# Hybrid attention and convolution trunk: values and compression with 64 stationary columns and two heads in turn, transposes in two banks, the conformer's statistics and the output banks placed anew

## The chip, the cores and the metric

The kernel runs on one core of one Trainium2 chip, as one launch over the whole trunk. The metric is the device time of a run in microseconds (us); the number quoted for a kernel is the median of three runs. Beside the runs stands one profiled execution, in which the hardware profiler recorded the instructions of every engine. The engines are PE (TensorE, matmuls; PEld is its weight loads), DVE (VectorE), ACT (ScalarE), POOL (GpSimd) and SP (SyncE, which here only queues the DMAs of the weights). Matmul results land in eight banks of PSUM, here bank 0 to bank 7; in the lists of instructions further down they are named bank_64 to bank_71.

## What is computed

One layer on 256 tokens of 2048 channels, in float32:

```
h    = rms_norm(x, mix_norm_g)
proj = h @ w_in                      # q 1024, k/v of 3 branches x 4 kv heads x 64, gates 48, conv 2048 columns
attn = nsa_attention(q, kv, sigmoid(gates), rel_bias, cmp_pos, cmp_w1, cmp_w2)   # 16 q heads, 4 kv heads
conv = conformer_conv(conv_in, conv_w, conv_b, conv_ln_g, conv_ln_b)
x    = x + concat([attn, conv]) @ w_out
x    = x + conv_glu_ffn(rms_norm(x, ffn_norm_g), w_up, ffn_conv_w, ffn_conv_b, w_down)
out  = rms_norm(x, final_norm_g)

def compress_tokens(tok, pos, w1, w2):     # blocks of 32 tokens, a step of 16 apart: 15 blocks a head
    blocks = <overlapping blocks of tok> + pos
    return silu(flat(blocks) @ w1) @ w2

def conformer_conv(h2, conv_w, conv_b, ln_g, ln_b):
    a, gate = split(h2, 2)
    u = causal_depthwise_conv(a * sigmoid(gate), conv_w, conv_b)    # 31 taps, 1024 channels
    return silu(layer_norm(u, ln_g, ln_b))                          # mean and variance over the channels
```

The attention of each head is the gated sum of three softmax attentions, all with a bias by relative position: over the 15 compressed blocks, over selected blocks of 64 tokens, and over a window. At 256 tokens all blocks are selected and the window covers everything, so the last two differ only in their keys and values.

## The kernel before

**Arithmetic.** Every large projection is done in high and low parts: a value is split into a part `h` rounded to the matmul's format and the rest `l`, and a product is three matmuls, h·h, h·l and l·h (`mm3`, lines L142 to L144; rows form in L149 to L151, and L615 to L617 for the values and gates). Such a matmul is one record in the trace. Plain float32 matmuls (value products, transposes by an identity, statistics) may show as two records, "passes". The weights come in chunks of 1 MB through SP's queue; ACT rounds them (`wh`, L110) and DVE or, for chunks 5 to 30, POOL makes the rest (`wl`, L115), some of it between the matmuls of the chunk ahead.

**Order.** PE's order is written out by hand. It takes the chunks in turn: 16 for the conformer's gates and values (GLU), 4 for the keys and values that get compressed, 4 for the other keys (k), 2 for the values of one branch (v), 4 for the values of the other with the gates (vg), 8 for the queries (q), 16 for the output projection (each a quarter of the output columns `qr` by a group `g` of 4 k-tiles, in an order `OUT_ORDER`), then 88 and 44 for the feed-forward part. `w_next` brings in the next chunk and runs what was left for "late", the copies out of the banks of the chunk before.

Each chunk calls `hook` four times. A hook runs: the attention ticks that `TICKS` gives it; what stands in `behind`; one piece of a weight split; one `step`, which takes one entry each from the lists `conf` (the conformer's statistics) and `steps` (compression, the compressed branch, residuals); and `fill`, which issues convolution taps while a running estimate of DVE's clock is not far ahead of PE's. An empty entry (`lambda: None`) in a list delays what is behind it by one hook.

**Convolution.** For each of 8 blocks of 128 channels, 30 taps are DVE instructions (L368) on an accumulator in bank 6 or 7; the last one writes `y[:, j]`. As soon as no tap is left, `conf_steps` starts the layer norm: `conf_sum` reduces `y` over the 8 blocks on DVE (L426), the mean is two matmuls against `inv_c` (L430), then subtract (L457), square on ACT, reduce again, the variance by four small matmuls (L437), a power on POOL (L467), a diagonal (L443), spread over the rows by two matmuls (L446), a multiply. Later come the SiLU and the split into `cf["o"]`. All of these use one corner of bank 6.

**Compression.** `cmp_in` (L517) multiplies the 16 position pairs of all four heads against the k weights and the v weights side by side: 128 stationary columns and 150 moving ones (75 for k, 75 for v), of which two diagonal quarters are used. The moving columns are picked out of `tok` with a step of 8. `cmp_sig` and `cmp_silu` form the hidden layer `hd`, `cmp_out` the second step (L540 for k, L544 for v).

**Attention** is a pipeline over 32 units: 8 pairs of heads `i`, the head `r` of the pair, the branch `br`. Tick n issues, in this order: `st_out` of unit n-6, `st_transpose` of n-5 (three transposes into bank 6), `st_scores` of n (banks 2, 4, 5), `st_rec` of n-3, `st_min` of n-1 (bias and row minimum, DVE), `st_evac` of n-5 (ACT's copy `es` of the transposed weights, 2 buffers), `st_scale` of n-3 (POOL), `st_exp` of n-1 (ACT). `st_out` is two value matmuls into bank 7: the stationary is `v[:, 0]`, 128 columns wide, in which `vt` holds the 64 values of head r and 64 zeros, so that the two heads of a pair add up in the upper and the lower rows of bank 7. The pair's last unit adds the compressed branch and splits bank 7 into `ma_h` and `ma_l`.

The compressed branch has its scores (`cmp_scores`) and the transposes of its weights `pcb` (`cmp_tr`, L685) in bank 3. The output projection's rows are in banks 0 and 1, 2 and 3, 4 and 5, 6 and 7 (`ob`); attention runs on into its first chunks, and loops ahead of output chunks 1, 3 and 6 force what is still left.

## Time and profile before

| | |
|---|---|
| runs | 1134.94 us median of 3 (1134.56 to 1135.63) |
| profiled execution | span 1135.5 us |
| PE | 1113.0 us busy, 98% of the span, 6482 matmul records |
| PEld | 976.3 us busy, 86% |
| DVE | 768.0 us busy, 68%, 1252 instructions |
| ACT | 579.2 us busy, 51%, 836 instructions |
| POOL | 187.1 us busy, 16%, 144 instructions |
| HBM | 204.27 MB read, 182 GB/s over the span |

The record of the profiled execution names no time for it beyond its span, so this is its own time; it lies 0.6 us above the median of the runs. How to read the rows: matmuls are pipelined, so the duration of one (some 0.28 us for 256 columns) is longer than the distance between the starts of two (0.12 us), and it is the distance that PE's path is made of. In a list in order of time the columns are the start and the duration in us, the engine, the line, the operation, what it writes and reads, its shape (stationary rows by columns, then rows by moving columns) and, in brackets, how long the engine had been idle and what it waited for. `xN` at a row's end counts the records taken together.

### The profile page before, as it was taken

To read this page: it belongs to the slowest core of one execution; us is meant where nothing else is said; L and a number is where in the kernel's file an instruction comes from. 1 tells how busy PE (TensorE), PEld (TensorE's weight loads), DVE (VectorE), ACT (ScalarE), POOL (GpSimd) and SP (SyncE) were. 2 spreads that over 40 slices of the span, in tenths; PEclk is the share of its full clock that TensorE was granted. 3 is DMA by queue.
4 is the path that set the end of the run, shared out by engine and by line. 5 is a ranking of instruction groups with operands and counts; after the bars stand their busy time and mean duration, and the time that the engine had idled before them with its cause. 6 is when DMAs were issued, how large, how long until landed. Compare 5 with 4: busy or idle time off the path is not lost.

```text
span 1135.5 us, 16238 instructions
## 1 busy us (share of the span) xinstructions
PE 1113.0 (98%) x6482; PEld 976.3 (86%) x6482; DVE 768.0 (68%) x1252; ACT 579.2 (51%) x836; POOL 187.1 (16%) x144
## 2 busy tenths in 40 slices
PE   8999997999999999999999999999999999999997
PEld 8999997999788888888888888888888888888886
DVE  7699676766455677777777777777777645556554
ACT  7444255677564555555545555554555444444442
POOL 0888666356500000000000000000000000000000
PEclk9999998999999999999999999999999999999999
DMA  9585424422354555555555555555555454555541
GB/s 374 212 289 207 159 89 153 146 75 111 120 215 156 210 199 195 197 194 186 185 186 190 188 193 198 191 190 185 186 185 191 182 191 182 195 185 188 188 165 75
DMA packets 32425, 207.46 MB, mean 183 GB/s; under 512 B 3883, under 2 KB 6203, under 8 KB 8284
## 3 DMA queue, kind: packets, MB, share of 16 engines
q1 hardware_dynamic: 28972, 199.85, 48.7%
q10 hardware_dynamic: 3376, 6.55, 1.6%
q8 instruction: 51, 0.84, 0.3%
q14 instruction: 26, 0.21, 0.1%
HBM read 204.27 MB, written 2.12 MB: 182 GB/s over the span
## 4 chain that ended last, share of the span: by engine, by line
PE 91%; DVE 4%; ACT 2%; POOL 1%; issue 1%; DMA 1%; SPq 0%; DVEq 0%; POOLq 0%; ACTq 0%
PE bank L976 29%; PE bank L994 21%; PE bank L978 14%; PE bank L142 5%; PE bank L144 5%; PE bank L143 5%; PE bank L151 3%; PE bank L149 3%; PE bank L150 3%; DVE bank L368 2%; PE bank L766 1%; PE bank L753 1%; DMA hb<-in_head 1%; PE bank L517 1%; POOL wl L115 1%
## 5 line engine op out<-in xcount | busy, mean ns | idle before, releaser
L110 ACT ACTIVATE wh<-wraw 128x2048 fp32r<-128x2048 f32 (+2 forms) x239 | 355.6, 1505 | 375.7 <-issue 143.8
L115 DVE TENSOR_TENSOR wl<-wraw,wh 128x2048 fp32r<-128x2048 f32 (+1 forms) x185 | 363.3, 1970 | 201.8 <-ACT wh L110 201.6
L976 PE MATMUL bank<-xt,wh 128*128 128x512 f32 x1408 | 488.6, 394 | 0.0
L978 PE MATMUL bank<-xt,wl 128*128 128x256 f32 x1408 | 390.1, 277 | 0.0
L976 PEld LDWEIGHTS bank<-xt,wh 128*128 128x128 f32 x1408 | 264.0, 188 | 61.1
L978 PEld LDWEIGHTS bank<-xt,wl 128*128 128x128 f32 x1408 | 264.4, 188 | 0.0
L142 PE MATMUL bank<-xt,wh 128*128 128x256 f32 x512 | 147.6, 288 | 2.5 <-ACT wh L243 2.5
L144 PE MATMUL bank<-xt,wl 128*128 128x256 f32 x512 | 145.8, 285 | 0.3 <-DVE wl L244 0.2
L143 PE MATMUL bank<-xt,wh 128*128 128x256 f32 x512 | 145.5, 284 | 0.0
L178 POOL TENSOR_TENSOR rstd<-ms,half 128x1 f32<-128x1 f32 x4 | 2.2, 553 | 821.0 <-DVE ms L171 821.0
L115 POOL TENSOR_TENSOR wl<-wraw,wh 128x1024 fp32r<-128x1024 f32 (+1 forms) x54 | 121.1, 2272 | 43.0 <-ACT wh L110 42.0
L994 PE MATMUL bank<-wh,gl 128*128 128x512 f32 x336 | 106.0, 396 | 0.0
L994 PE MATMUL bank<-wh,gh 128*128 128x512 f32 x336 | 106.0, 396 | 0.0
L994 PE MATMUL bank<-wl,gh 128*128 128x512 f32 x336 | 106.0, 396 | 0.0
L142 PEld LDWEIGHTS bank<-xt,wh 128*128 128x128 f32 x512 | 98.5, 192 | 4.2 <-ACT wh L243 2.9
L144 PEld LDWEIGHTS bank<-xt,wl 128*128 128x128 f32 x512 | 98.3, 192 | 0.7 <-DVE wl L244 0.7
L143 PEld LDWEIGHTS bank<-xt,wh 128*128 128x128 f32 x512 | 98.5, 192 | 0.5
L368 DVE SCALAR_TENSOR_TENSOR bank<-us,cw,bank 128x256 f32<-128x256 f32 x232 | 95.4, 482 | 3.5 <-ACT bank L363 2.9
L939 DVE SCALAR_TENSOR_TENSOR yt<-u,vecs,yt 128x255 f32<-128x255 f32 (+1 forms) x176 | 80.9, 480 | 3.1
L994 PEld LDWEIGHTS bank<-wh,gl 128*128 128x128 f32 x336 | 63.3, 188 | 15.4
L994 PEld LDWEIGHTS bank<-wl,gh 128*128 128x128 f32 x336 | 63.3, 188 | 15.4
L994 PEld LDWEIGHTS bank<-wh,gh 128*128 128x128 f32 x336 | 63.2, 188 | 15.4
(191 smaller groups left out, 1117.1 us busy)
## 6 DMA issues: line engine op xcount, KB each, us to landing
wraw<-in_w_u SPq DMA_DIRECT2D x88, 1024.0 KB, 4.8
wraw<-in_w_d SPq DMA_DIRECT2D x44, 1024.0 KB, 4.7
wraw<-in_w_t SPq DMA_DIRECT2D x30, 1024.0 KB, 4.9
wraw<-in_w_o SPq DMA_DIRECT2D x16, 1024.0 KB, 4.8
wraw<-in_w_vg SPq DMA_DIRECT2D x4, 608.0 KB, 3.8
hb<-in_head SPq DMA_DIRECT2D x2, 1024.0 KB, 10.3
xr<-in_x SPq DMA_DIRECT2D x2, 1024.0 KB, 18.9
wb<-rel_scratch ACTq DMA_DIRECT2D x1, 2048.0 KB, 10.8
```

The source lines that it names most:

```text
L110: nc.scalar.activation(h[:, sl], raw[:, sl], AF.Copy)
L115: (nc.gpsimd if pooled else nc.vector).tensor_sub(l[:, sl], raw[:, sl], h[:, sl].bitcast(F32))
L142: nc.tensor.matmul(ps, wh, xh, start=first, stop=False)
L143: nc.tensor.matmul(ps, wh, xl, start=False, stop=False)
L144: nc.tensor.matmul(ps, wl, xh, start=False, stop=last)
L149: nc.tensor.matmul(ps, xh, wh, start=first, stop=False)
L150: nc.tensor.matmul(ps, xh, wl, start=False, stop=False)
L368: nc.vector.scalar_tensor_tensor(y[:, j] if last else acc[0], us[:, j, k:k + T], cw[:, j, k:k + 1], acc[0], op0=OP.mult, op1=OP.add)
L939: nc.vector.scalar_tensor_tensor(ys[i][:, d:], us_[i][:, :T - d], fcw[:, c, k:k + 1], ys[i][:, d:], op0=OP.mult, op1=OP.add)
L976: nc.tensor.matmul(bk[i], wh[:, k, sl], xt[:, kt].rearrange("p a t -> p (a t)"), start=kt == 0, stop=False)
L978: nc.tensor.matmul(bk[i][:, :T], wl[:, k, sl], xt_h[:, kt], start=False, stop=kt == KD - 1)
L994: nc.tensor.matmul(banks[n], g[p][:, kt % 4, sl], ws[w][:, k * 1024 + n * 512:k * 1024 + (n + 1) * 512], start=kt + i == 0, stop=i == 2 an ...
```

## The change

- **Values.** `vt` loses its zeros; a stationary is 64 columns wide. `st_out` does nothing for r = 0, and for r = 1 it issues the products of both heads, in turn, into rows 0 to 63 and 64 to 127 of bank 7: four matmuls a branch, eight passes. Since it needs both heads' `es`, it comes a tick later (DEEP = 7), and `es` has 5 buffers instead of 2.
- **Compression.** `cmp_in` does the same with k and v: 32 matmuls of 64 stationary and 75 moving columns in place of 16 of 128 and 150. It stands behind 6 empty steps instead of 2, and `cmp_out` behind 5 instead of 1.
- **Transposes** go to banks 3 and 6 in turn. The compressed branch moves its scores to bank 1 and its transposes to bank 0 (bank 5 for the last group, m = 3, which also gets two empty steps instead of none ahead of its transposes).
- **Conformer's statistics.** `ysum` is added up on DVE as each block's taps end (`conf_add`). `conf_center` is put in ahead of q chunk 1: one matmul for the mean (both halves of the tokens at once, bank 0, `ones` with the factor in ACT's copy), subtraction in four pieces, squares by ACT in four pieces, added up by DVE. `conf_norm` is put in ahead of output chunk 2: variance (two matmuls against a column of `ones`), power, diagonal, one spread matmul, all in bank 6, with empty steps between; then multiply, SiLU and split.
- **Output banks.** `ob` becomes (0,1), (4,2), (5,3), (6,7); output chunks have their own ticks in `TICKS`, and the forcing loops become assertions.
- **Small tiles.** The table of the feed-forward taps, `fcw`, gets a tile of its own and is loaded at the start of the feed-forward part, on ACT's queue ahead of `gfin`; `inv_c` and the clearing of the zeros in `vt` (POOL) are gone.

```
-        vt = ap.tile([P, 2, 2, 2, 3, HD], F32, name="vt")
-        nc.gpsimd.memset(vt[:, :, :, :, 1], 0.0)
+        vt = ap.tile([P, 2, 2, 2, 2, HD], F32, name="vt")
...
         def st_out(n):
             i, r, br = units[n]
-            es = US.pop(n)
-            o, v = bank[7], vt[:, :, br, i // 4, r:r + 2]
+            if r == 0:
+                return
+            es, o, q = [US.pop(n - 2), US.pop(n)], bank[7], i // 4
             kw = dict(skip_group_check=True)
-            nc.tensor.matmul(o[:, :T], v[:, 0], es[:, :T], start=r + br == 0, stop=False, **kw)
-            nc.tensor.matmul(o[:, P:T], v[:, 1], es[:, T:], start=False, stop=False, **kw)
-            if r == 1 and br == 1:
+            for b, cols in enumerate((slice(0, T), slice(P, T))):
+                for rr in range(2):
+                    nc.tensor.matmul(o[64 * rr:64 * rr + 64, cols], vt[:, b, br, q, rr],
+                                     es[rr][:, :T] if b == 0 else es[rr][:, T:], start=br + b == 0, stop=False, **kw)
+            if br == 1:
...
-        DEEP = D_T + 1
+        DEEP = D_T + 2
...
             for i in range(16):
-                nc.tensor.matmul(bank[4][:, :150], w1[:, i].rearrange("p v d -> p (v d)"), tok[:, :, :, i:i + 113:8],
-                                 start=i == 0, stop=i == 15)
+                for kv in range(2):
+                    nc.tensor.matmul(bank[4][64 * kv:64 * kv + 64, :75], w1[:, i, kv], tok[:, kv, :, i:i + 113:8],
+                                     start=i == 0, stop=i == 15)
...
-        steps.extend((lambda: None, lambda: None, cmp_in, lambda: None, lambda: cmp_sig(0), lambda: cmp_sig(1),
-                      lambda: cmp_silu(0), lambda: cmp_silu(1), lambda: None, cmp_out, lambda: None, cmp_keep))
+        steps.extend((*[lambda: None] * 6, cmp_in, lambda: None, lambda: cmp_sig(0), lambda: cmp_sig(1),
+                      lambda: cmp_silu(0), lambda: cmp_silu(1), *[lambda: None] * 5, cmp_out, lambda: None, cmp_keep))
...
+        def conf_add(j):
+            summed.append(j)
+            if len(summed) > 1:
+                nc.vector.tensor_add(ysum, y[:, summed[0]] if len(summed) == 2 else ysum, y[:, j])
...
+        def conf_mean():
+            cf["b"] = bank[0][:, :T]
+            nc.tensor.matmul(cf["b"], ones, ysum, start=True, stop=True)
+            conf_keep(1.0 / NCONV)
...
+        def conf_center():
             conf.extend((
-                lambda: None, lambda: conf_sum("y", y, 0, P), lambda: conf_sum("y", y, P, T), lambda: None,
-                lambda: None, lambda: conf_mean(0), lambda: conf_mean(1),
-                lambda: (conf_apply(OP.subtract, 0), conf_sq(0)), lambda: conf_apply(OP.subtract, 4),
...
+                no, no, conf_mean, no, lambda: conf_apply(OP.subtract, 0), lambda: conf_apply(OP.subtract, 2),
+                lambda: conf_sq(0, 0), lambda: (conf_sq(2, 2), conf_apply(OP.subtract, 4)),
+                lambda: conf_apply(OP.subtract, 6), lambda: conf_fold(2, 2),
+                lambda: conf_sq(4, 2), no, lambda: conf_fold(2, 2), lambda: conf_sq(6, 2), no,
+                lambda: conf_fold(2, 2), no, lambda: conf_fold(1, 1)))
+        def conf_norm():
+            conf.extend((
+                no, no, conf_var, no, conf_rstd, no, conf_diag, no, conf_spread, no,
...
-            es = wk.tile([P, 384], F32, name="es", bufs=2)
-            nc.scalar.activation(es, bank[6][:, :384], AF.Copy)
+            es = wk.tile([P, 384], F32, name="es", bufs=5)
+            nc.scalar.activation(es, bank[TR_BANKS[n % 2]][:, :384], AF.Copy)
...
-        TICKS = {0: {}, 1: {2: 1, 3: 1}, 2: {0: 1, 1: 1, 2: 1, 3: 1}, 3: {0: 1, 1: 2, 2: 1, 3: 2}}
+        TICKS = {0: {}, 1: {2: 1, 3: 1}, 2: {0: 1, 1: 1, 2: 1, 3: 1}, 3: {0: 1, 1: 1, 2: 1, 3: 2}, 4: {0: 1, 1: 1, 2: 1, 3: 2}, 5: {0: 1, 1: 1, 2: 1}}
...
-            if i == 2:
+            if i == 1:
                 fill(1e9)
+                conf_center()
...
-        ob = [bank[0:2], bank[2:4], bank[4:6], bank[6:8]]
+        ob = [[bank[b] for b in p_] for p_ in ((0, 1), (4, 2), (5, 3), (6, 7))]
...
+        fcw = fp.tile([P, 2 * NFT, 4], F32, name="fcw")
+        nc.scalar.dma_start(fcw.rearrange("p t k -> p (t k)"), a["vecs"][:, KD:])
```

In the lists below a row is an instruction: its line, operation, what it writes and reads, and its shape (for a matmul, stationary columns by moving columns; otherwise partitions by elements); x6 stands for six alike in a row.

**Place 1, the mean of the layer norm.** PE before: the mean (L430) stands among the value-and-gate matmuls of the vg chunks (L615 to L617).

```order
L617 MATMUL bank_67<-wh,xt 128x304
L430 MATMUL bank_70<-y,inv_c 128x128
L615 MATMUL bank_66<-wh,xt 128x304
L616 MATMUL bank_66<-wl,xt 128x304
L617 MATMUL bank_66<-wh,xt 128x304
```

PE now: it stands in q chunk 1 (L142 to L144), behind the first scores of attention (L712, L713).

```order
L144 MATMUL bank_65<-xt,wl 128x256
L712 MATMUL bank_66<-k_h,qs 128x256
L713 MATMUL bank_66<-k_l,qs 128x256
L712 MATMUL bank_68<-k_h,qs 128x512
L713 MATMUL bank_68<-k_l,qs 128x512
L430 MATMUL bank_64<-ysum,ones 128x256
L142 MATMUL bank_65<-xt,wh 128x256
```

So it moved past the rest of vg and q chunk 0, and covers both halves of the tokens at once.

DVE before, at the end of the convolution: the last taps of the last two blocks (L368, writing `y`), then the reductions over the blocks (L426) and the subtraction (L457).

```order
L368 SCALAR_TENSOR_TENSOR bank_71<-us,cw,bank_71 128x256
L368 SCALAR_TENSOR_TENSOR y<-us,cw,bank_70 128x256
L368 SCALAR_TENSOR_TENSOR bank_71<-us,cw,bank_71 128x256 x6
L368 SCALAR_TENSOR_TENSOR y<-us,cw,bank_71 128x256
L426 TENSOR_REDUCE y<-y 128x128 x2
L457 TENSOR_TENSOR y<-y,ck 128x1024 x2
```

DVE now, at the same end of the convolution (the taps are L369 here, the addition L354); behind it come the small operations of the gates.

```order
L369 SCALAR_TENSOR_TENSOR y<-us,cw,bank_70 128x256
L354 TENSOR_TENSOR ysum<-ysum,y 128x256
L369 SCALAR_TENSOR_TENSOR bank_71<-us,cw,bank_71 128x256 x6
L369 SCALAR_TENSOR_TENSOR y<-us,cw,bank_71 128x256
L354 TENSOR_TENSOR ysum<-ysum,y 128x256
L626 TENSOR_SCALAR alive<-wb 128x1
L627 TENSOR_SCALAR gates<-gates,alive 128x16
```

The two reductions are replaced by an addition behind the last tap of each block but the first, and the subtraction is no longer next in line.

**Place 2, the values.** PE before, a tick of attention inside a q chunk: the value matmuls (L766, L767), the transposes (L753), the scores (L711, L712).

```order
L144 MATMUL bank_65<-xt,wl 128x256
L766 MATMUL bank_71<-es,vt 128x256
L767 MATMUL bank_71<-es,vt 128x128
L753 MATMUL bank_70<-ident,e 128x128 x3
L711 MATMUL bank_66<-k_h,qs 128x256
L712 MATMUL bank_66<-k_l,qs 128x256
L711 MATMUL bank_69<-k_h,qs 128x512
L712 MATMUL bank_69<-k_l,qs 128x512
L142 MATMUL bank_65<-xt,wh 128x256
```

PE now, a tick with values (L770; the transposes are L754).

```order
L144 MATMUL bank_65<-xt,wl 128x256
L770 MATMUL bank_71<-es,vt 64x256 x2
L770 MATMUL bank_71<-es,vt 64x128 x2
L754 MATMUL bank_67<-ident,e 128x128 x3
L142 MATMUL bank_65<-xt,wh 128x256
```

Two units' value matmuls now stand together, 64 columns wide, and the transposes go to bank 3 or bank 6; scores follow in every second tick with values (not in this one), and ticks without values remain between them.

**Place 3, the second step of compression.** PE before: `cmp_out` (L540, L544) stands in a k chunk.

```order
L143 MATMUL bank_66<-xt,wh 128x256
L144 MATMUL bank_66<-xt,wl 128x256
L540 MATMUL bank_69<-hd,w_101 64x30 x2
L544 MATMUL bank_68<-w_101,hd 32x64 x8
L142 MATMUL bank_66<-xt,wh 128x256
```

PE now: it stands among the value matmuls of v (L601 to L603).

```order
L602 MATMUL bank_65<-wl,xt 128x256
L603 MATMUL bank_65<-wh,xt 128x256
L541 MATMUL bank_69<-hd,w_99 64x30 x2
L545 MATMUL bank_68<-w_99,hd 32x64 x8
L601 MATMUL bank_64<-wh,xt 128x256
```

It moved back by the eight empty steps that were added ahead of it, four of them ahead of the first step: two chunks.

More of the change, by code (lines that the diff above doesn't have):

```diff
@@ L338, in hook @@
             fill(1.0 if i in ticks else 0.8 if cbst["q"] else 2.0)
-            if not side and cbst["glu"] and "b" not in cf:
-                conf_steps()
         def tile_chunk(ps, ticks={}):
@@ new lines, in conf_spread, with conf_apply, conf_sq @@
+        def conf_spread():
+            nc.tensor.matmul(cf["b"], ones, cf["d"].rearrange("p t c -> p (t c)"), start=True, stop=True)
+            conf_keep()
+        def conf_apply(op, j0, n=2):
+            nc.vector.tensor_tensor(y[:, j0:j0 + n], y[:, j0:j0 + n], cf["k"][:, None].to_broadcast([P, n, T]), op=op)
+        def conf_sq(j0, at):
+            if j0 == 0:
+                cf["s"] = ap.tile([P, 4, T], F32, name="s2", tag="tok")
+            nc.scalar.activation(cf["s"][:, at:at + 2], y[:, j0:j0 + 2], AF.Square)
@@ L441, in conf_diag, with conf_fold, conf_rstd @@
+        def conf_fold(lo, n):
+            nc.vector.tensor_add(cf["s"][:, :n], cf["s"][:, :n], cf["s"][:, lo:lo + n])
+        def conf_rstd():
+            rv = wk.tile([P, 2], F32, name="rv", bufs=1)
+            nc.vector.tensor_scalar(rv, cf["b"][:, :2], 1.0 / NCONV, EPS, op0=OP.mult, op1=OP.add)
+            for t in range(2):
+                nc.gpsimd.tensor_tensor(rv[:, t:t + 1], rv[:, t:t + 1], half, op=OP.pow)
+            cf["r"] = rv
+        def conf_diag():
             cf["d"] = wk.tile([P, 2, P], F32, name="dg", bufs=1)
@@ L442, in conf_diag @@
             for t in range(2):
-                nc.vector.tensor_scalar_mul(cf["d"][:, t], ident, cols[:, t:t + 1])
-        def conf_spread(t):
-            nc.tensor.matmul(cf["b"], ones, cf["d"][:, t], start=True, stop=True)
-            conf_keep(t)
-            if t:
-                cf["done"] = True
-        def conf_keep(t):
-            if t == 0:
-                cf["k"] = wk.tile([P, T], F32, name="ck", tag="sg")
-            nc.scalar.activation(cf["k"][:, t * P:(t + 1) * P], cf["b"], AF.Copy)
@@ L846, in hybrid_trunk @@
             if n == 1:
[L847 to L850 removed]
+                assert tick["n"] > NU - 2
             if n == 2:
```

87 lines of the change are left out of this document (27 added, 60 removed).

## The prediction

> **What bounds the kernel now.** I read the page first, then busy time cut at the places where TensorE (PE) changes its kind of work, then PE in order of time around each of these cuts.
>
> ```profile
> span 1135.5 us, 16238 instructions
> PE 1113.0 (98%) x6482; PEld 976.3 (86%) x6482; DVE 768.0 (68%) x1252; ACT 579.2 (51%) x836; POOL 187.1 (16%) x144
> ```
>
> PE is busy 98% of the span, so the change gains only where it takes matmul time away or a wait of PE. The next rows are the stretches: compression and k (127.23), v (160.94), v with gates, vg (172.46), the first q chunks (195.13), attention beside q (206.01), attention beside the output projection (277.81), the rest of that projection (309.28), and the feed-forward part (389.76). Columns: from and to, length, then busy time of PE, PEld, DVE, ACT, POOL, then PE's granted clock.
>
> ```profile
> 127.23:160.94 33.71, 32.59 (x247) 30.27 (x246) 19.43 (x53) 13.95 (x24) 19.25 (x13) 1.00 0.30 100
> 160.94:172.46 11.52, 11.52 (x99) 11.52 (x98) 10.15 (x26) 6.72 (x15) 5.70 (x5) 1.00 0.30 108
> 172.46:195.13 22.67, 17.78 (x110) 17.45 (x109) 15.57 (x19) 10.24 (x15) 14.51 (x10) 0.85 0.44 156
> 195.13:206.01 10.88, 10.04 (x84) 9.84 (x83) 7.13 (x12) 6.93 (x17) 3.48 (x4) 1.00 0.71 255
> 206.01:277.81 71.80, 71.32 (x543) 68.26 (x542) 46.25 (x179) 52.96 (x153) 39.81 (x47) 1.00 0.25 89
> 277.81:309.28 31.47, 28.60 (x163) 24.01 (x161) 15.74 (x61) 18.95 (x54) 19.25 (x21) 1.00 0.28 103
> 389.76:1135.50 745.74, 737.25 (x3909) 628.09 (x3907) 503.08 (x596) 362.49 (x406) 2.21 (x4) 1.00 0.52 185
> ```
>
> The v stretch is the measure of a full PE: 96 matmuls of 256 columns in 11.52 us, 0.12 each. The feed-forward stretch, 746 us, keeps its instructions; only its small table of taps is loaded elsewhere. So everything happens between 127 and 309 us.
>
> **The conformer's statistics** (place 1 of the change). PE stands still inside vg, and again later:
>
> ```profile
> 174.97 0.30 PE L615 MATMUL bank<-wh,xt 128*128 128x304 f32 x1
> 175.66 0.30 PE L617 MATMUL bank<-wh,xt 128*128 128x304 f32 x1
> 179.95 0.79 PE L430 MATMUL bank<-y,inv_c 128*128 128x128 f32 x2 [3.99 <-DVE y L426]
> 181.05 0.46 PE L617 MATMUL bank<-wh,xt 128*128 128x304 f32 x1
> 181.30 0.46 PE L615 MATMUL bank<-wh,xt 128*128 128x304 f32 x1
> 191.87 0.83 PE L437 MATMUL bank<-inv_c,s 128*128 128x1 f32 x6 [0.90 <-DVE s L426]
> 192.56 0.39 PE L615 MATMUL bank<-wh,xt 128*128 128x304 f32 x1
> 198.29 0.49 PE L446 MATMUL bank<-dg,ones 128*128 128x128 f32 x2 [0.84 <-DVE dg L443]
> 177.48 0.48 DVE L368 SCALAR_TENSOR_TENSOR y<-us,cw,bank 128x256 f32<-128x256 f32 x1
> 177.99 3.74 DVE L426 TENSOR_REDUCE y<-y 128x128 f32<-128x1024 f32 x2
> ```
>
> The matmul of the mean is queued on PE in the middle of vg, while VectorE (DVE) still has taps until 177.96 and then two reductions of 3.74 us. PE waits 3.99 us, and after it the vg matmuls start 0.25 us apart (181.05 to 181.30) instead of 0.14 (174.97 to 175.66 is five starts): the granted clock of this stretch is 0.85. Then come the waits for the sum of squares (0.90) and for the diagonal (0.84).
>
> After the change vg holds none of this: 96 matmuls at 0.138 are 13.25 us, so 22.67 - 13.25 = **9.4 us go**. The stretch behind it holds 78 matmuls (48 and 30) of 0.12 = 9.36 us, and of its 10.88 the other **1.5 go**. What comes back elsewhere on PE: one matmul of the mean over 256 columns and one of the spread, each in two passes that I take at 0.215 (see the values below), 0.43 each, and four passes of the variance at 0.115 (191.87 to 192.56 is six starts), 0.46: **1.3 us come back**.
>
> Do these wait in their new place? The mean now stands behind the first scores of q chunk 1. PE gets there at about 206 less the gains ahead of it (9.4, 1.5, 1.3, 4.1) and 0.7 of scores, near 190. DVE ends its taps at 177.96 before; it takes on seven additions of 128x256, 0.42 each by its nearest row (the subtraction of that shape, below), 2.9 us at most at the end: 181, nine microseconds early. The four reductions leave DVE (3.74, and two more over squares), and the sums of squares move beside attention: ACT does them in four pieces instead of two, DVE adds with four instructions. Of the subtraction, the squaring and the folding nothing is on PE's path, since the variance is asked for only in output chunk 2, after eighteen steps. The variance, the power, the diagonal and the spread stand two hooks apart, 2.8 us of matmuls each; the wait they replace was for a chain of that length squeezed together. I cost them at nothing; if this cover is gone, the 0.84 comes back.
>
> **Compression.** Its two steps on PE:
>
> ```profile
> 130.99 8.68 PE bank L517 x32
> 149.46 0.28 PE L144 MATMUL bank<-xt,wl 128*128 128x256 f32 x1
> 149.67 0.30 PE L540 MATMUL bank<-hd,w 64*64 64x30 f32 x4
> 151.10 0.45 PE L544 MATMUL bank<-w,hd 64*32 64x64 f32 x16 [1.12 <-DVE hd L533]
> 151.48 0.39 PE L142 MATMUL bank<-xt,wh 128*128 128x256 f32 x1
> 66.42 0.28 PE L144 MATMUL bank<-xt,wl 128*128 128x256 f32 x1
> 66.63 0.81 PE L292 MATMUL bank<-oh,rbn 33*16 33x384 f32 x2
> 67.38 0.39 PE L142 MATMUL bank<-xt,wh 128*128 128x256 f32 x1
> 67.60 0.28 PE L143 MATMUL bank<-xt,wh 128*128 128x256 f32 x1
> ```
>
> The second step waits for its hidden layer: between the two groups 1.43 us pass where about 0.1 is work. With five empty steps instead of one it stands in v, some 3 us of PE and many taps later: **1.3 us go**.
>
> The first step, 32 passes in 8.68 us, becomes 64 passes of half the moving columns, for k and for v in the two halves of the array. Do two halves run at the same time? L544 answers for quarters: sixteen passes of 64 columns, each 64/256 of 0.215 = 0.054, would take 0.86 one after another; the matmul behind them starts 0.38 after the first of them (151.10 to 151.48). So narrow tiles overlap. They also cost at entry and exit: L292, with 16 columns, starts 0.21 after the matmul ahead of it (normally 0.12), and the matmuls behind are back in step at 67.48 (67.60 less 0.12), 0.85 after 66.63 for 2 x 384 columns that stream in 0.65 at the rate of the 0.215: 0.09 + 0.20 = 0.29 a visit. In the Trainium skill, the page "TensorEngine Tiling (Array Packing)", section "Tiling Modes", states that a change of the tiling mode empties the engine first; by that rule every visit pays, and the trace agrees with the 0.29. A reader who took switches as free would forecast 4.9 us less (rival 1).
>
> With overlap the first step is 4.34 + 0.29 = 4.6: **4.1 us go**. Bounds: no overlap, 8.68 + 0.29, a loss of 0.3; no price of the switch, 4.3 gained. I take the overlap, by L544, the nearest row with several column tiles.
>
> **Values** (place 2). One unit's two value matmuls are four passes:
>
> ```profile
> 245.85 0.59 PE L766 MATMUL bank<-es,vt 128*128 128x256 f32 x2
> 246.28 0.38 PE L767 MATMUL bank<-es,vt 128*128 128x128 f32 x2
> 246.50 0.49 PE L753 MATMUL bank<-ident,e 128*128 128x128 f32 x3
> ```
>
> They hold PE from 245.85 to 246.50, 0.65 us (0.215 a pass of 256 columns, 0.11 of 128): 32 units, 20.8 us. The stationary is 128 wide today with half of it zeros. The change feeds two heads side by side: sixteen groups of eight passes, four in each half. Overlapped, a group takes 0.65 and a visit 0.29: 16 x 0.94 = 15.0. **5.8 us go.** Bounds: nothing overlaps, 16 x 0.29 = 4.6 lost; free switch, 10.4 gained. Smaller weight loads (64 columns) lie under the passes.
>
> **Transposes, banks, distances.** The three transposes keep their work. With two banks, five buffers and outputs up to two ticks behind the copy, these waits lose their cause:
>
> ```profile
> 217.79 0.28 PE L144 MATMUL bank<-xt,wl 128*128 128x256 f32 x1
> 218.55 0.70 PE L766 MATMUL bank<-es,vt 128*128 128x256 f32 x2 [0.48 <-ACT es L758]
> 283.14 0.49 PE L753 MATMUL bank<-ident,e 128*128 128x128 f32 x3
> 284.27 0.70 PE L766 MATMUL bank<-es,vt 128*128 128x256 f32 x2 [0.64 <-ACT es L758]
> 293.62 0.40 PE L151 MATMUL bank<-wh,ma_l 128*128 128x512 f32 x1
> 296.25 0.44 PE L685 MATMUL bank<-ident,pcb 128*128 128x128 f32 x2 [2.23 <-DVE pcb L680]
> 290.34 1.22 DVE L115 TENSOR_TENSOR wl<-wraw,wh 128x1024 fp32r<-128x1024 f32 x1
> L721 DVE CUSTOM_DVE_ANT_0 e<-bank,wb 128x256 f32<-128x256 f32 x32 | 13.4, 419 | 0.0
> L773 DVE TENSOR_TENSOR ma_l<-bank,ma_h 128x256 fp32r<-128x256 f32 x7 | 3.0, 425 | 11.4 <-ACT ma_h L772 11.4
> ```
>
> Start to start, less the normal distance, PE loses 0.64, 0.80 (283.14 plus three transposes of 0.11) and 2.39 (the compressed weights of the last head group, now two steps further off): 3.8. What is late next: output chunk 1 now takes bank 4 and then bank 2, and bank 2 is free only when DVE has done both last minima. Between the two banks DVE has a split of 1.22, two minima (0.42 for the larger half, less for the smaller: some 0.8 each) and eight small steps, which I put at 1.4: 4.2 in all, an estimate. PE has twelve row matmuls of 0.23 (512 columns at the 0.12 of 256) and two transpose sets of 0.33: 3.4. I take 0.8 back. The feed-forward part opens in banks 2 and 3, and bank 3 now holds a transposed quarter; its copies are asked for fifteen row matmuls (3.5 us) earlier, which covers four short instructions: nothing. **3.0 us go**; bounds 3.8, and minus 2.4 where one more wait as long as the longest appears.
>
> Does another engine become the bound beside attention? ACT is busy 52.96 of 71.80 us, and takes on some 3 us of squares and copies; PE falls to about 67: 56 of 67. POOL 39.81 and DVE 46.25 are further off. The clearing of the zeros leaves POOL. The taps' table is queued on ACT right ahead of the final norm's vector, more than two feed-forward chunks ahead of its first reader; it costs ACT an issue, PE nothing.
>
> **Sum**, from the profiled 1135.5: 9.4 + 1.5 - 1.3 + 1.3 + 4.1 + 5.8 + 3.0 = 23.8, so 1111.7. The median of the runs, 1134.94, lies 0.6 under that span: **1111 us**.
>
> **Rivals.**
> 1. Switches are free. For it: entry and exit were measured with fewer rows than 128, and the value tiles keep all rows. Then 17 x 0.29 = 4.9 more go: 1106.
> 2. The first compression step gains nothing, because its moving columns are picked with a step of eight elements: 8.68 / 32 = 0.271 a pass of 150 columns is 1.8 ns a column, against 0.84 in the contiguous 0.215 of 256. If fetching is the limit and both halves share it, 4.4 less go: 1115. The Trainium skill, "SBUF — State Buffer", section "Door 1: The DMA port swizzle", has memory lines of 16 bytes and a penalty for each access that leaves one; the row agrees that such reading is slow, and does not tell whether two streams share the penalty.
> 3. Halves do not overlap: the change then saves no PE time, and its switches cost. 23.8 - 4.4 - 5.8 - 4.6 = 9.0 go: 1126. Against it: L544.
> 4. Slower: emptying PE costs far more around a full-height tile, with queues of attention restarted sixteen times. Without any switch 28.7 go; seventeen visits eat this at 1.7 us each. At 2 us: 1140. The nearest row says 0.29.
>
> **Chances.** Forecast 0.55, rival 1 0.13, rival 2 0.18, rival 3 0.09, rival 4 0.02; 0.03 for waits in attention beyond these. A measurement here can tell about 0.2%, 2.3 us, from no change. The forecast's own range is 1108 to 1115; the full one takes in rival 1 with all 3.8 of waits gone (1105) and rival 2 without any gain in the waits and one new (1122). Faster 0.96, same 0.02, slower 0.02.
>
> **What would show it.** vg one stretch near 13.3 us at clock 1.00 with no statistics in it; the first compression group near 4.6 (8.9 would be rival 2); value groups holding PE about 0.94 (0.65 rival 1, 1.6 rival 3); no wait of PE for the copies `es` or for `pcb`, and one below 1 us for the minima near output chunk 1. A wait of PE for the mean, or for the taps' table, would break the sum.

## The result, and the profile after

The changed kernel takes 1115.9 us (median of 4 runs, 1115.07 to 1116.73) against 1135.18 of the kernel before: a ratio of 0.9832, 95% interval 0.982 to 0.9844. Forecast were 1111 (1105 to 1122): the direction and the range hold, but of the 23.8 us that were to go, 19.3 went. One run each of e7 and e8 below, far longer at a lower mean clock (1538.75 and 1361.57 us at 0.654 and 0.752), is left out of their figures.

With the runs came the span of each: a run's time is 1.8 us above its span, and the nine runs of before that stood beside the first experiments had a median of 1135.02 at spans of 1133.1 to 1133.6. The profile of before that was shown (1135.5) was thus one of its longer executions, which by the same 1.8 took some 1137.3: it is 2.3 us behind the changed kernel already at 36 us, partly by half clock (a granted clock of 0.66 from 15 to 20 us). The gains below are reckoned without these. From 1133.2 to 1113.3, the span after, are 19.9.

The page of the changed kernel, busy time by engine:

```profile
span 1113.3 us, 16297 instructions
PE 1098.0 (99%) x6506; PEld 956.6 (86%) x6506; DVE 770.4 (69%) x1262; ACT 577.6 (52%) x836; POOL 188.1 (17%) x143
```

Busy time of the stretches that answer to those of before: vg, the first q chunks up to the first scores, attention beside q, attention beside the output projection up to the variance, and the feed-forward part.

```profile
164.98:178.36 13.38, 13.38 (x98) 13.38 (x97) 8.03 (x18) 7.69 (x11) 11.22 (x8) 1.00 0.68 235
178.36:187.72 9.36, 9.36 (x80) 9.36 (x79) 7.04 (x7) 5.98 (x14) 4.43 (x3) 1.00 0.77 266
187.72:259.49 71.77, 67.88 (x535) 61.06 (x534) 51.43 (x192) 54.79 (x159) 43.44 (x49) 1.00 0.28 99
259.49:290.52 31.03, 30.80 (x189) 22.61 (x187) 14.60 (x55) 20.59 (x58) 15.86 (x20) 1.00 0.39 143
368.53:1113.30 744.77, 736.33 (x3909) 627.21 (x3907) 503.40 (x596) 362.57 (x406) 2.19 (x4) 1.00 0.52 186
```

vg is one full stretch at clock 1.00, the stretch behind it is 78 matmuls of 0.12, and the feed-forward part is 0.97 shorter than before. Attention beside q is where the forecast fails: 71.77 us as before (71.80), though its value matmuls take less; PE is busy in 67.88 of them where it was in 71.32. What stands still there and in the first output chunks (the last row), PE in order of time, only rows with a wait (in brackets: idle time and what ended it):

```profile
201.23 0.35 PE L712 MATMUL bank<-k_h,qs 128*128 128x256 f32 x1 [0.68 <-DVE mn L722]
203.93 0.44 PE L754 MATMUL bank<-ident,e 128*128 128x128 f32 x2 [0.22 <-POOL e L748]
208.22 0.36 PE L712 MATMUL bank<-k_h,qs 128*128 128x256 f32 x1 [2.09 <-DVE mn L722]
231.65 0.36 PE L712 MATMUL bank<-k_h,qs 128*128 128x256 f32 x1 [0.45 <-DVE mn L722]
255.09 0.36 PE L712 MATMUL bank<-k_h,qs 128*128 128x256 f32 x1 [0.45 <-DVE mn L722]
266.35 0.50 PE L149 MATMUL bank<-wh,ma_h 128*128 128x512 f32 x1 [0.23 <-DVE ec L667]
```

Four times the scores (L712) wait for a row minimum `mn` on DVE. Start to start, beyond the normal distance, the six are 0.84, 0.38, 2.25, 0.61, 0.61 and 0.39: 5.1 us. None of the first five was there before. The engines around the longest of them, in order of time:

```profile
203.62 0.42 DVE L722 CUSTOM_DVE_ANT_0 e<-bank,wb 128x256 f32<-128x256 f32 x1
204.14 0.49 ACT L733 ACTIVATE e<-e,mn 128x256 f32<-128x256 f32 x1
204.63 0.84 ACT L644 ACTIVATE qs<-q 64x256 fp32r<-64x256 f32 x2
205.07 0.86 DVE L645 TENSOR_TENSOR qs<-q,qs 64x256 fp32r<-64x256 f32 x2 [1.02 <-ACT qs L644]
205.94 0.69 DVE L444 TENSOR_TENSOR y<-y,ck 128x512 f32<-128x512 f32 x1
206.55 0.27 DVE L677 TENSOR_REDUCE smc<-ec 128x8 f32<-128x120 f32 x1
207.29 0.28 DVE L680 TENSOR_TENSOR pcb<-ec,smc 128x120 f32<-128x120 f32 x1
207.78 0.28 DVE L722 CUSTOM_DVE_ANT_0 e<-bank,wb 128x128 f32<-128x128 f32 x1
```

DVE finishes one minimum, waits 1.02 for ACT, whose copies of q stand behind two exponentials, splits q, subtracts a piece of the conformer (L444), takes the steps of the compressed branch (`cmp_probs`, L677 to L680), and only then the minimum that PE waits for. PE meanwhile has no value matmuls at all: the first stand at 210.72, behind four sets of transposes (the first at 198.29), where in the kernel before they stand at 218.55, behind one set (216.15). So PE is through with its other work at 206. The wait of DVE for ACT in the split of q was there before the change, too:

```profile
221.74 0.86 DVE L645 TENSOR_TENSOR qs<-q,qs 64x256 fp32r<-64x256 f32 x2 [1.02 <-ACT qs L644]
```

The groups that were to shrink, PE in order of time:

```profile
134.34 4.61 PE L518 MATMUL bank<-tok,w 128*64 128x75 f32 x64
138.88 0.39 PE L142 MATMUL bank<-xt,wh 128*128 128x256 f32 x1
154.91 0.30 PE L541 MATMUL bank<-hd,w 64*64 64x30 f32 x4
155.14 0.45 PE L545 MATMUL bank<-w,hd 64*32 64x64 f32 x16
155.52 0.39 PE L601 MATMUL bank<-wh,xt 128*128 128x256 f32 x1
210.51 0.28 PE L144 MATMUL bank<-xt,wl 128*128 128x256 f32 x1
210.72 0.87 PE L770 MATMUL bank<-es,vt 128*64 128x256 f32 x8
211.52 0.55 PE L754 MATMUL bank<-ident,e 128*128 128x128 f32 x3
```

The first compression step takes 4.61, the second no longer waits for its hidden layer, and a value group holds PE from 210.63 (0.12 behind L144) to 211.52: 0.89.

### The profile page after: what moved, and what is told of

Read it like the earlier page. It is cut to its first block, busy times and chain, and to the rows that moved or that the text cites. A ratio compares the mean times of both kernels' runs of the same rounds, so it can differ in the third digit from the quotient of the medians.

```text
span 1113.3 us, 16297 instructions
## 1 busy us (share of the span) xinstructions
PE 1098.0 (99%) x6506; PEld 956.6 (86%) x6506; DVE 770.4 (69%) x1262; ACT 577.6 (52%) x836; POOL 188.1 (17%) x143
## 4 chain that ended last, share of the span: by engine, by line
PE 93%; DVE 2%; ACT 1%; POOL 1%; DMA 1%; issue 1%; SPq 0%; POOLq 0%; DVEq 0%; ACTq 0%
PE bank L972 29%; PE bank L990 21%; PE bank L974 14%; PE bank L142 5%; PE bank L144 5%; PE bank L143 5%; PE bank L149 3%; PE bank L150 3%; PE bank L151 3%; PE bank L770 1%; POOL e L748 1%; DMA hb<-in_head 1%; PE bank L754 1%; ACT e L733 0%; PE bank L518 0%
## 5 line engine op out<-in xcount | busy, mean ns | idle before, releaser
L142 PE MATMUL bank<-xt,wh 128*128 128x256 f32 x512 | 146.7, 287 | 1.4 <-ACT wh L239 1.4
L144 PE MATMUL bank<-xt,wl 128*128 128x256 f32 x512 | 145.0, 283 | 0.3 <-DVE wl L240 0.2
L142 PEld LDWEIGHTS bank<-xt,wh 128*128 128x128 f32 x512 | 98.0, 191 | 3.2 <-ACT wh L239 1.9
L144 PEld LDWEIGHTS bank<-xt,wl 128*128 128x128 f32 x512 | 98.0, 191 | 0.7 <-DVE wl L240 0.7
L369 DVE SCALAR_TENSOR_TENSOR bank<-us,cw,bank 128x256 f32<-128x256 f32 x232 | 94.9, 482 | 2.8 <-ACT bank L364 2.1
L935 DVE SCALAR_TENSOR_TENSOR yt<-u,fcw,yt 128x255 f32<-128x255 f32 (+1 forms) x176 | 80.9, 481 | 3.1
```

Source lines behind the costliest of these rows:

```text
L142: nc.tensor.matmul(ps, wh, xh, start=first, stop=False)
L144: nc.tensor.matmul(ps, wl, xh, start=False, stop=last)
L369: nc.vector.scalar_tensor_tensor(y[:, j] if last else acc[0], us[:, j, k:k + T], cw[:, j, k:k + 1], acc[0], op0=OP.mult, op1=OP.add)
L935: nc.vector.scalar_tensor_tensor(ys[i][:, d:], us_[i][:, :T - d], fcw[:, c, k:k + 1], ys[i][:, d:], op0=OP.mult, op1=OP.add)
```

## The experiments

All are timed beside the kernel before (1134.76 to 1135.21 in median). The changed kernel and several of the others have two levels 1.6 us apart: 1115.1 (two runs) and 1116.7 (two). What the upper one is comes out of the profiles of two of them. Windows of one us each behind the wait near 206 (the number after the busy times is PE's granted clock), first the changed kernel at its lower level, then the kernel with the label e12_tap_table_early, profiled at its upper level:

```profile
209.00:210.00 1.00, 1.00 (x10) 1.00 (x9) 1.00 (x6) 1.00 (x4) 1.00 (x2) 1.00 0.00 0
211.00:212.00 1.00, 1.00 (x12) 0.76 (x9) 0.64 (x5) 1.00 (x4) 1.00 (x2) 1.00 0.00 0
```

```profile
209.00:210.00 1.00, 1.00 (x6) 0.80 (x5) 1.00 (x5) 1.00 (x3) 1.00 (x2) 0.50 0.00 0
211.00:212.00 1.00, 1.00 (x6) 1.00 (x6) 0.67 (x5) 1.00 (x4) 1.00 (x2) 0.50 0.00 0
```

After the same wait of 2.25 us PE's clock is halved in one execution and not in the other, and the matmuls start 0.213 apart until 212.0: some 1.6 us lost. Over the windows of that trace from 208 to 213 the shares (0.82, three times 0.50, 0.98) add up to 3.4 us of half clock. The Trainium skill, "TensorE: Matmul & The Clock Gate", section "Part 1: The HAM clock gate (the "warmup" mystery)", has a free-running window of about 3.4 us: after an idle one the clock is half, after a busy one full again. The 3.4 us agree. The idle time does not: by these rows a wait of 2.25 us was enough in one execution, well below a whole window, and not in the other. The clock of these two traces changes only at multiples of 3.41 us from its other changes (208.63, 212.04 and 1109.75 in e12). Counted back in such steps from 1108.12, where the clock of the changed kernel falls at its end, a border at 207.0 cuts its wait into 1.0 and 1.2, while in e12 the whole wait lies between 205.2 and 208.6. That would explain the difference, but it was not tested, and in e9 some 2.0 us of a wait lie in one step without half clock behind it. Below, kernels are compared at the lower level unless it says otherwise.

**e1: the conformer's pieces later.**

```diff
-                no, no, conf_mean, no, lambda: conf_apply(OP.subtract, 0), lambda: conf_apply(OP.subtract, 2),
+                no, no, conf_mean, *[no] * 14, lambda: conf_apply(OP.subtract, 0), lambda: conf_apply(OP.subtract, 2),
```

> The changed kernel, with 14 empty steps between the mean and the conformer's subtraction, squares and additions, so that these stand in q chunks 5 to 7 and output chunk 0 instead of q chunks 2 to 4. Theory C (these pieces, 0.69 us each on VectorE and 0.61 on ACT, make the minima late for which PE's scores wait): the three waits of PE near 200.3, 203.4 and 205.9 us (0.84, 0.38, 2.25 beyond the normal distance, 3.5 in all) go or shrink below 1 us in all, and the time falls by 2.5 to 3.5, to 1112.4 to 1113.4. Theory B (the two lean ticks without value matmuls let PE run into the minima, behind the compressed branch and the split of q): the waits stay, with the 0.6 us ones near 231 and 254: 1115.9 within 0.6. If the pieces only take their delay along, new waits of that size stand in q chunks 5 to 7.

Measured: 1113.85 (ratio 0.9813, 0.98 to 0.9826). Its profiled execution has 4 us of waits ahead of all this that the other runs lack (1118.0 of span against 1112.0; half clock behind one of them takes the rest), so only its stretch of attention is read: 0.84 and 0.38 are gone, 2.25 is 1.47, the two 0.61 stand, and the wait at the first output chunks grew from 0.39 to 0.99, where the last pieces now stand. 5.1 became 3.7. Theory C holds for 2.0 us and not for the rest, and 0.6 of new wait takes part of it back.

**e2: values one tick later.**

```diff
-        DEEP = D_T + 2
+        DEEP = D_T + 3
-... 5: {0: 1, 1: 1, 2: 1}}
+... 5: {0: 1, 1: 1, 2: 1, 3: 1}}
```

> The changed kernel, with the value matmuls one tick later (DEEP 8), so that they stand in the two ticks before the one whose scores wait, and not one tick earlier; the copies of the weights still have five buffers, now all in use. Theory B: the waits of 0.6 us near 231 and 254 go, and most of the 2.25 near 206, since PE arrives 0.9 us later there: 1.2 to 2.5 less, 1113.4 to 1114.7. Theory C: the 2.25 loses only the 0.9 by which PE comes later and the other value ticks get waits in exchange: 1115 to 1116.

Measured: 1115.28 (0.9827, 0.9814 to 0.9841). The two 0.61 are gone, as theory B has it. But 0.84, 0.38 and 2.25 stand unchanged: before PE's first value group (210.72 in the changed kernel) there is nothing to come later. And 0.45 and 0.77 of new waits follow, for the compressed branch and at the first output chunks. Lost and won cancel.

**e3: the small clearing on DVE.**

```diff
-            nc.gpsimd.memset(e[:, 0, :, NC0:], BIG)
+            nc.vector.memset(e[:, 0, :, NC0:], BIG)
```

> The changed kernel, with the small clearing in the compressed branch (128x32) done by VectorE in place of POOL, where it stands behind four scalings of attention. Theory P (VectorE's idle time for that clearing, 1.20 us near 200 and 2.8 us in all three times, sets the wait of 0.84 of PE near 200.3): that wait goes and the later ones shrink, 0.8 to 1.5 us less, 1114.4 to 1115.1. Theory C alone: VectorE's idle time is filled by work that is due anyway, and the time stays within 0.4 of 1115.9.

Measured: 1114.53 (0.9822, 0.9809 to 0.9836). The 0.84 is gone, 0.38 is 0.28, the rest stands, one wait grew by 0.28: 0.6 less, as the waits sum up (5.1 to 4.4). DVE's wait for POOL was on PE's path in the first group alone.

**e4: the two halves one after the other.**

```diff
-            for b, cols in enumerate((slice(0, T), slice(P, T))):
-                for rr in range(2):
+            for rr in range(2):
+                for b, cols in enumerate((slice(0, T), slice(P, T))):
...
-            for i in range(16):
-                for kv in range(2):
+            for kv in range(2):
+                for i in range(16):
```

> The changed kernel, with the same narrow matmuls in another order: first both of one head, then both of the other; in compression first the 16 of k, then the 16 of v. Theory N (the two halves of the array run together only for neighbours in PE's queue): a value group grows from 0.65 us of passes to about 1.08 (only the first head's short passes lie beside the second head's long ones), 16 times 0.43 = 6.9 us, and the first compression step from 4.3 to 8.6: 11 us more, 1127, less what of it only fills the waits near 200 to 206. Theory F (any two matmuls of different halves overlap, whatever their order): within 0.5 us of 1115.9.

Measured: 1120.52 (0.9869, 0.9856 to 0.9883); 3.8 above the changed kernel's upper level, where three of its four runs lie. Neither theory. Compression's first step and a value group in its trace:

```profile
134.25 8.44 PE L518 MATMUL bank<-tok,w 128*64 128x75 f32 x64
215.78 0.28 PE L144 MATMUL bank<-xt,wl 128*128 128x256 f32 x1
215.99 0.88 PE L770 MATMUL bank<-es,vt 128*64 128x256 f32 x8
216.80 0.44 PE L754 MATMUL bank<-ident,e 128*128 128x128 f32 x2
```

Compression lost 3.8 of the 4.3 of theory N, and the values next to nothing: 215.99 to 216.80 is 0.81, 210.72 to 211.52 was 0.80. In the single starts of a value group the four passes of 256 columns come first, in pairs 0.013 us apart, and then the four of 128, although one head's two of 128 stand ahead of the other's of 256 in the order; in compression 28 passes start alone, then come four pairs whose starts lie 0.006 to 0.021 us apart, then 28 alone. The records don't name k and v; by the count the pairs are the last four of k with the first four of v. So a pass for the other half is taken out of turn and runs beside one that stands four places ahead of it. A head of a unit has just four passes; k has 32.

**e5: cmp_probs one hook earlier.**

```diff
-  (lambda m: None, cmp_scores, cmp_exp, lambda m: None, cmp_probs, lambda m: None, cmp_tr)
+  (lambda m: None, cmp_scores, cmp_exp, cmp_probs, lambda m: None, lambda m: None, cmp_tr)
```

> The changed kernel, with the five small VectorE steps of the compressed branch (cmp_probs) one hook earlier for the first three head groups, so that they no longer stand right behind the split of q, where VectorE has just waited 1.02 us for ACT. Theory S (split of q and cmp_probs fall into the same hook, ahead of the minima that the next scores wait for): both 0.6 us waits near 231 and 254 go, and the 2.25 near 206 shrinks by about 1.2, the length of the five steps; 2.0 to 2.4 less, 1113.5 to 1113.9. Theory C (the conformer's pieces alone): the 2.25 stays and only the 0.6s change, 1114.7 to 1115.9.

Measured: 1115.71, all four runs within 0.2 (0.9829, 0.9816 to 0.9843). The two 0.61 became 0.35 and nothing, but the 2.25 stands: DVE takes the same steps, now ahead of the copy of q, and comes to the minimum no earlier. The waits fell by 0.9, and its profile has the half clock after the 2.25 (0.50 at 211 to 212); with all runs on one level it seems to come in each, which takes the 0.9 back.

**e6: the three together**: the edits of e3 and e5, and the pieces nine hooks later in place of thirteen, so that they end in q chunk 7. Only this last edit is shown.

```diff
-                no, no, conf_mean, no, lambda: conf_apply(OP.subtract, 0), ...
+                no, no, conf_mean, *[no] * 10, lambda: conf_apply(OP.subtract, 0), ...
```

> The changed kernel with cmp_probs one hook earlier, the small clearing on VectorE, and the conformer's pieces nine hooks later, so that they end inside q chunk 7. If theories S, C and P each own their share, all waits of PE for the minima (0.84, 0.38, 2.25, 0.61, 0.61: 4.7 us) go but for some 0.5: 1111.5 to 1112. If the pieces take their delay along into q chunks 4 to 7, 1113 to 1114.

Measured: 1112.16, all runs within 0.3 (0.9799, 0.9785 to 0.9812). Waits of 1.10, 0.52, 0.27 and 0.40 are left, 2.3 of 5.1, and no upper level. The rest of theory S, the split of q that waits for ACT, is still there.

**e7: transposes in one bank.**

```diff
-        TR_BANKS = (3, 6)
+        TR_BANKS = (6, 6)
```

> The changed kernel with all transposes in bank 6, as before the change; five buffers and the later values stay. If the second bank is what took the waits for the copies away, PE's transposes now wait for the copy of the tick before: a copy takes 0.47 us and stands on ACT behind two exponentials, and the lean ticks are 1.8 us apart: waits of 0.3 to 0.6 in some of the 32 ticks, 1 to 4 us more, 1117 to 1120. If the later values alone did it, 1115.9 within 0.5.

Measured: 1115.79 and three times 1117.2 to 1117.4 (0.9841, 0.9827 to 0.9854). In the groups of waits of PE in attention, the waits change their name:

```profile
PE bank L754 <- ACT es L759: 3.6, 5, 1.3
PE bank L712 <- DVE mn L722: 0.5, 1, 0.5
```

Transposes wait 3.6 us for the copies, five times, but mostly where the scores would have waited a moment later: 0.7 us worse at the lower level. The second bank does what was forecast of it, and in this kernel it is worth less than 1 us. The profile, at the upper level, has half clock (0.50 from 210 to 212) behind two waits of 1.31 and 0.69 us, which stand only one set of transposes apart.

**e8: the kernel before, its statistics moved alone.**

```diff
-            if not side and cbst["glu"] and "b" not in cf:
-                conf_steps()
...
-            if i == 2:
+            if i == 1:
                 fill(1e9)
+                conf_steps()
```

> The kernel before, with one thing changed: the conformer's statistics, in their old form, are started ahead of q chunk 1 and not as soon as the taps are out. By the forecast's first term vg loses 9.4 us and the stretch behind it 1.5, and the 16 passes come back as matmul time (eight of 0.11 for mean and spread, eight of 0.11 for the variance: 1.8): 9.1 less than the 1135.0 of before, 1126. If the reductions (3.74 us) and the subtraction in one piece (1.3), now on VectorE beside the first ticks of attention, hold up the minima as the pieces of the changed kernel do, 2 to 5 us of it are lost again: 1128 to 1131.

Measured: 1137.2 (1.0021, 1.0012 to 1.0031), slower than before. Its vg, and its waits of PE from there to the middle of the output projection (us in total, times, longest):

```profile
170.11:183.49 13.38, 13.38 (x98) 13.38 (x97) 5.34 (x13) 7.69 (x11) 12.69 (x9) 1.00 0.66 236
```

```profile
PE bank L764 <- ACT es L756: 3.7, 6, 1.2
PE bank L683 <- DVE pcb L678: 2.2, 1, 2.2
PE bank L444 <- ACT es L756: 1.8, 2, 0.9
PE bank L428 <- ACT ck L452: 1.1, 1, 1.1
PE bank L709 <- DVE mn L719: 0.9, 2, 0.4
```

vg shrinks just as in the changed kernel, and everything is lost again in attention. The old statistics use a corner of bank 6, so the second half of the mean waits until ACT has copied the first out (L428), the spread waits for the copies of the transposes there (L444), and the values wait for copies behind them (L764). The 2.2 for `pcb` is a wait of the kernel before. The first term of the sum is therefore no gain of the place alone. That it takes the small pieces and the other banks is read from these waits; no run has the one without the other.

**e9: values 128 columns wide again.**

```diff
-                    nc.tensor.matmul(o[64 * rr:64 * rr + 64, cols], vt[:, b, br, q, rr],
+                    nc.tensor.matmul(o[:, cols], vt[:, b, br, q, rr:rr + 2],
```

> The changed kernel with the value stationaries 128 columns wide again, zeros in one half, the eight passes of a group at the same place and in the same order, each over the whole array; the copies have four buffers in place of five, to make room. By the forecast a group goes from 0.65 us of passes and 0.29 for the switch to 1.30: 16 times 0.36 = 5.8 us more; by the trace of the changed kernel (a group holds PE some 0.89 us with its entry and exit) 16 times 0.4 = 6.5 more. Of that the waits behind lean ticks (two of 0.6) may fill 0 to 1.2: 1121 to 1122.5. If the halves had gained nothing, 1115.9 or less.

Measured: 1120.5 (0.9872, 0.9858 to 0.9885); profiled 1118.5 against 1113.3: the pairing is worth 5.2. A group here (the matmul behind it is the next transpose):

```profile
210.64 1.47 PE L771 MATMUL bank<-es,vt 128*128 128x256 f32 x8
211.95 0.49 PE L755 MATMUL bank<-ident,e 128*128 128x128 f32 x3
```

1.31 us against 0.89 (from 0.12 behind the matmul ahead to the next), and 0.05 to 0.1 of that comes back in the matmul behind the narrow group, which takes longer to get going. The waits are those of the changed kernel (5.0).

**e10: the split of q ahead of the tick**, on top of e6.

```diff
+            while behind:
+                behind.pop(0)()
             if i in ticks:
                 for _ in range(ticks[i]):
                     attn_tick()
-            while behind:
-                behind.pop(0)()
```

> The kernel with the three moves (label e6_all_three, 1112.16 us) and one more: in each hook what stands in the list behind, the split of q, is issued ahead of the attention tick and not behind it. Theory S in its narrower form (VectorE stands idle 1.02 us in each split of q because ACT has two exponentials ahead of its copies, and the minima behind it are what PE's scores wait for): ACT's copies then come first, the idle time goes, and PE's remaining waits for minima near 204, 228 and 252 (1.10, 0.52, 0.27) shrink to 0.2 or less: 1110.3 to 1110.8. If the order only moves the idle time (ACT's exponentials 0.9 us later, the scalings and transposes behind them later too), 1112 to 1113.

Measured: 1111.51 (0.979, 0.9777 to 0.9804). 0.52, 0.27 and 0.40 are gone; the one near 204 is 1.47 and not 0.2:

```profile
206.12 0.38 PE L712 MATMUL bank<-k_h,qs 128*128 128x256 f32 x1 [1.30 <-DVE mn L722]
```

**e11: cmp_probs behind these minima**, on top of e10. The lines are shown against the changed kernel; in e10 `cmp_probs` stood right behind `cmp_exp`.

```diff
-  (lambda m: None, cmp_scores, cmp_exp, cmp_probs, lambda m: None, lambda m: None, cmp_tr)
+  (lambda m: None, cmp_scores, cmp_exp, lambda m: None, lambda m: None, cmp_probs, cmp_tr)
```

> The kernel with the split of q first (label e10_split_first, 1111.5 us), with cmp_probs two hooks later, so that it stands behind the minima for which PE waits 1.47 us near 204.5, and right ahead of its own transposes. If the five steps of cmp_probs ahead of the copy and the split of q are what makes these minima late, the 1.47 falls to about 0.3 and PE waits up to 0.5 for the transposes instead: 0.7 to 1.2 less, 1110.3 to 1110.8. If the minima are late for the split of weights (1.22) that stands ahead of all of it, 1111.2 to 1111.8, with 0.5 of new wait for the transposes.

Measured: 1111.06 (0.9788, 0.9774 to 0.9801), the quickest. The 1.47 is 0.54 and the transposes wait in exchange:

```profile
205.25 0.38 PE L712 MATMUL bank<-k_h,qs 128*128 128x256 f32 x1 [0.37 <-DVE mn L722]
206.60 0.44 PE L685 MATMUL bank<-ident,pcb 128*128 128x128 f32 x2 [0.38 <-DVE pcb L680]
```

**e12: the taps' table back in its old place.**

```diff
+    vecs = consts.tile([P, KD + 4 * 2 * NFT], F32, name="vecs")
+    ffn_g = vecs[:, :KD]
+    fcw = vecs[:, KD:].rearrange("p (t k) -> p t k", k=4)
...
-        fcw = fp.tile([P, 2 * NFT, 4], F32, name="fcw")
```

> The changed kernel, with the table of the feed-forward taps back in the tile beside ffn_g and loaded early, as before the change; the copies of the weights have four buffers in place of five, to make room. In the forecast this edit costs and gains nothing; but the down projection's 1008 matmuls are 235.2 us long after the change (from the first start to the last) and 236.2 before. If the tile's place or its load is the cause, they are 236.2 again and the time is 0.9 higher, 1116 to 1116.8 where the other runs of the changed kernel have 1115.1; if something else is, 235.2 and no difference, 1115.1 within 0.5 in its quicker runs.

Measured: 1116.02, at its lower level 1115.9 to 1116.0 (0.9834, 0.9821 to 0.9848). The feed-forward stretch, and one of the three kinds of matmul in the down projection in before, in the changed kernel and here (durations in ns, least, median and most, then the first and the last start in us):

```profile
370.08:1115.80 745.72, 737.24 (x3909) 628.10 (x3907) 503.28 (x596) 362.58 (x406) 2.19 (x4) 1.00 0.52 185
```

```profile
L994 PE MATMUL bank<-wh,gl x336: 392/397/400, 880.6 to 1115.6; 128*128 128x512 f32 x168
L990 PE MATMUL bank<-wh,gl x336: 393/395/397, 859.5 to 1093.5; 128*128 128x512 f32 x168
L991 PE MATMUL bank<-wh,gl x336: 392/397/400, 860.9 to 1095.9; 128*128 128x512 f32 x168
```

745.72 again, as before (745.74). From the first matmul of the down projection to the last of the kernel it is 247.29 us here and in before, 246.28 in the changed kernel. The four buffers are not the cause: e9 has them too, with the table in its new tile, and takes 246.28. Nor is the load: the table is loaded long before, and only its last readers (up to 870.0 in the changed kernel) fall into these 246 us. That leaves where the tiles lie: with the table among them or not, those of the feed-forward part should stand at other addresses. The traces don't show addresses, and which tile matters was not tried, so this cause is argued and not shown.

The waits of PE in attention (start to start beyond the normal, those over 0.2, without stretches of half clock) account for the times of the kernels that differ from the changed one in order or engine only, but for e5 (4.2 us of waits, so 1114.2, and 1115.7 measured, with the half clock):

| kernel | waits, us | 1115.1 less the change of the waits | measured |
|---|---|---|---|
| changed | 5.1 | | 1115.1 |
| e2 | 5.1 | 1115.1 | 1115.3 |
| e3 | 4.4 | 1114.4 | 1114.5 |
| e1 | 3.7 | 1113.7 | 1113.85 |
| e6 | 2.3 | 1112.3 | 1112.2 |
| e10 | 1.5 | 1111.5 | 1111.5 |
| e11 | 1.3 | 1111.3 | 1111.1 |

## Why the prediction was right, and where a step failed

The terms, forecast and measured in PE's starts from before to after:

| term | forecast | measured |
|---|---|---|
| statistics out of vg | 9.4 | 9.3 |
| out of the stretch behind it | 1.5 | 1.5 |
| back elsewhere (mean 0.43, variance 0.45, spread 0.43) | -1.3 | -1.3 |
| `cmp_out` waits no more | 1.3 | 1.2 |
| `cmp_in` in two halves | 4.1 | 3.95 |
| values in two halves | 5.8 | 5.2 (e9) |
| waits in attention | 3.0 | -1.3 |
| taps' table | 0 | 1.0 (e12) |
| sum | 23.8 | 19.6 of the 19.9 |

- **Overlap and switch.** Halves run together (starts of a pair 0.006 us apart), and a visit costs about what L292 gave, 0.29: a value group holds PE for 0.24 more than its passes (0.89 against 0.65), and costs 0.05 to 0.1 more behind it. Rival 1 (free) and rival 3 (no overlap) fall. Rival 2 falls too: a pair of strided passes takes 0.137 for 75 columns each, 1.8 ns a column as in before, with both halves reading at once.
- **The mean** stands in its new place without a wait (L713 at 188.19, L430 at 188.42), as reckoned.
- **The step that failed** is the waits. The old ones did go (0.64, 0.80, 2.39). "What is late next" was looked for at the row banks, where it is 0.39 for a forecast 0.8, and "Of the subtraction, the squaring and the folding nothing is on PE's path" looked at the variance alone. These pieces are on the path by another door: in DVE's order of instructions the minima that the scores wait for stand behind them (205.94 and 207.78 in the rows above). Two things that the profile of before showed were not put together: DVE's 1.02 us of waiting in each split of q, and that attention's ticks, at DVE's pace with a little slack, would get two leaner ones in four, and three more without values at the start, once the values stand in pairs. Moving the conformer's pieces (e1) removes 2.0 us of these waits and brings 0.6 back elsewhere, moving the clearing (e3) removes 0.7; the first wait, 0.84, goes in either, so the two are not a sum. e6, e10 and e11 take out 3.8 of the 5.1. In the sum the term was 3.0 and came out at -1.3; with the values (0.6 short) and the table (1.0 not forecast) this is nearly the whole difference. The remaining 1.3 of e11 are for a minimum (0.54) and for the compressed branch's weights (0.54 and 0.23).
- **The median** lies another 0.8 above the lower level, because half of the runs pay 1.6 us of half clock behind the longest wait (read from e12's profile at its upper level; no upper run of the changed kernel was profiled). The forecast priced a wait at its own length only.
- The busy shares that were to rule out another bound (ACT 56 of 67) were nearly right, 54.8 of 67.9, and beside the point: no engine was full, one chain was late.
- That e11 comes out at the forecast 1111 is in part chance, since it has the table's 1.0 that was not in the sum. The upper end of the range, 1122, is not quite the sum that it names: 1115.4 and 5.4 of waits (3.0 lost, 2.4 new) are 1120.8.
- A slip in the words on the kernel: POOL makes `wl` for chunks 5 to 31, not 30; nothing rests on it.

## What to carry to other kernels

When work is moved off one engine's path to lie beside a pipeline, list for each engine, in its order of instructions, what will stand ahead of the instruction that the bottleneck waits for, tick by tick; a busy share of 70% says nothing on that. Making the bottleneck's work shorter in some ticks and not in others turns the slack of its partners into waits there, so the freed time is only kept if their order is changed with it. And a wait of two us on PE may cost more than itself.

## What the runs showed of the hardware that was not expected

- Passes for the other half of the array start out of turn, beside passes that stand four places ahead of them (e4): for short runs the order of issue between two halves did not matter, for 32 passes in a row it cost 3.8 us.
- Half clock of 3.4 us can follow a wait of 2.25 us (e12) or two of 1.31 and 0.69 close together (e7); with single waits of 1.5 and less the runs of e6, e10 and e11 show none.
- With the table of the feed-forward taps in a tile of the feed-forward part, and not beside `ffn_g` at the start, the down projection took 246.28 us in place of 247.29, 0.4% less, with the same instructions; that the place of the tiles does it is the reading left, and not shown.
